# Low parts of weights made by an accumulating transfer in the mLSTM branch's projection

## The chip, the cores and the metric

The kernel runs on one core of one Trainium2 chip. The metric is device time in microseconds. The engines are TensorE (PE, with its weight loads as PEld), VectorE (DVE), ScalarE (ACT), GpSimd (POOL) and SyncE (SP), which here only issues transfers.

## What is computed

One layer of a streaming encoder on 256 tokens of width 2048. The input is normalised and goes through one wide projection. One branch is an mLSTM with 8 heads, the other a pooling mixer; each is multiplied by its own gate, projected back to 2048, and the two are merged by sigmoid gates. An output projection, a norm and the residual end the layer. The part that matters here is the first line below: `y_a` (256 x 2048) times `w_proj_mlstm` (2048 x 2048).

```
br_a = jnp.einsum('bsc,cd->bsd', y_a, w_proj_mlstm[l])
br_b = jnp.einsum('bsc,cd->bsd', y_b, w_proj_pool[l])
merged = jax.nn.sigmoid(g_a) * br_a + jax.nn.sigmoid(g_b) * br_b
out = jnp.einsum('bsd,de->bse', merged, w_out[l])
x = x + _rmsnorm(out, norm_post_w[l])
```

## The kernel before, in words

Every large product is made in three parts. Each factor is split into a high part (the value rounded to TensorE's float32r) and a low part (what is left), and high x high, low x high and high x low are summed in PSUM.

All weights stream from HBM. A raw tile of 128 x 2048 float32 (1 MB) is loaded by SP into one of three buffers (`rawp`, L49; the load is L102). It is cut into two halves of 1024 columns. For each half, `hi_lo` (L58) makes the high part `wh` by a copy on ACT (L61) and the low part `wl` by a subtraction on DVE, raw minus high (L62). `wh` and `wl` each have four buffers (`split`, L51), so ACT and DVE can be four halves ahead of PE, and a buffer comes free when PE has used it.

`tok_block` (L112) makes one 256 x 512 block of a product with tokens on the partitions: for each half first eight products with `wh` (L124 with the activations' high part, L125 with their low part), then four with `wl` (L127). The activations are the stationary operand. `chan_block` is its counterpart for products with channels on the partitions.

The order of the work is the order of the code: every engine runs its own queue in order and waits on semaphores for the others. Side jobs are generators that are advanced once per half (`step`, L78).

The last third of the kernel is a loop over four blocks of 512 output columns (j, L611). Each pass makes two gate blocks (L614, eight halves each), the pooling branch's projection (L625, four halves) and the mLSTM branch's projection (L630, four raw tiles, so eight halves), and then merges them on DVE (L635, L636). After the fourth pass comes the output projection (L684), whose weights have four further buffers for `wh` and `wl` in a pool of their own (`osplit`), so that ACT and DVE can start on them while PE is still in the fourth mLSTM projection.

GpSimd does little: constants at the start, the power -1/2 of the norms (L194, L666), and one addition for each token tile at the end (L672). Before the change no transfer is issued from it.

Of the kernel before, what the change touches and what calls it, by code (L numbers as in the profile page):

```python
# [10 lines left out]
F32 = mybir.dt.float32  # L11
F32R = mybir.dt.float32r
BF16 = mybir.dt.bfloat16
AF = mybir.ActivationFunctionType
ALU = mybir.AluOpType
AX = mybir.AxisListType

P = 128
# [20 lines left out]
def block_kernel(ctx: ExitStack, tc: tile.TileContext, a: dict, out: bass.AP):  # L39
# [3 lines left out]
    nc = tc.nc  # L43
# [5 lines left out]
    rawp = ctx.enter_context(tc.tile_pool(name="rawp", bufs=3, side="right"))  # L49
    gate = ctx.enter_context(tc.tile_pool(name="gate", bufs=2))  # L50
    split = ctx.enter_context(tc.tile_pool(name="split", bufs=4))  # L51
# [6 lines left out]
    def hi_lo(hi, lo, src, scale=None):  # L58

        if scale is None:  # L60
            nc.scalar.copy(hi, src)  # L61
            nc.vector.tensor_tensor(lo, src, hi.bitcast(F32), op=ALU.subtract)  # L62
        else:
            nc.scalar.activation(hi, src, AF.Copy, scale=scale)
            nc.vector.scalar_tensor_tensor(
                lo, src, scale, hi.bitcast(F32), op0=ALU.mult, op1=ALU.subtract
            )
# [10 lines left out]
    def step():  # L78
        side[:] = [g for g in side if next(g, None) is not None]

    def drain():
        while side:
            step()
# [14 lines left out]
    def w_tile(src, cuts=(0, 1024, 2048), pre=None, pool=split):  # L98

        raw = rawp.tile([P, 2048], F32, name="raw")  # L100
        if pre is None:
            nc.sync.dma_start(raw, src)  # L102
        for c0, c1 in zip(cuts, cuts[1:]):
            if pre is not None:
                pre(c0)
                nc.sync.dma_start(raw[:, c0:c1], src[:, c0:c1])
            wh = pool.tile([P, 1024], F32R, name="wh")
            wl = pool.tile([P, 1024], F32R, name="wl")
            hi_lo(wh[:, : c1 - c0], wl[:, : c1 - c0], raw[:, c0:c1])
            yield c0, c1, wh, wl  # L110

    def tok_block(tiles, st_h, st_l, opts=lambda kq: {}):  # L112

        ps = [acc.tile([P, 512], F32, name="acc") for _ in range(2)]
        n = 4 * len(tiles)
        for kq, src in enumerate(tiles):
            for c0, c1, wh, wl in w_tile(src, **opts(kq)):
                for part in range(2):
                    for c in range(c0, c1, 512):
                        k = kq * 4 + c // 512  # L120
                        cols = slice(c - c0, c - c0 + 512)
                        for t in range(2):
                            if part == 0:
                                nc.tensor.matmul(ps[t], st_h(k, t), wh[:, cols], start=k == 0, stop=False)  # L124
                                nc.tensor.matmul(ps[t], st_l(k, t), wh[:, cols], start=False, stop=False)  # L125
                            else:
                                nc.tensor.matmul(  # L127
                                    ps[t], st_h(k, t), wl[:, cols], start=False, stop=k == n - 1
                                )
                step()  # L130
        return ps
# [20 lines left out]
    def xtiles(b):  # L152
        return [a["wx"][b, i].rearrange("p k c -> p (k c)") for i in range(4)]
# [273 lines left out]

    side.append(stats())
    po = tok_block(xtiles(4), xh, xl, first)
    so0 = []  # L430
    for t in range(2):
# [12 lines left out]
    y_h = yp.tile([P, KT, T], F32R, name="y_h")  # L444
    y_l = yp.tile([P, KT, T], F32R, name="y_l")
# [119 lines left out]
    for j in range(4):  # L565
        po = tok_block(xtiles(4 + j), xh, xl) if j else so0
        so = []
        for t in range(2):
            s = gate.tile([P, 512], F32, name="g", tag=f"g{t}") if j else so0[t]
            nc.scalar.activation(s, po[t], AF.Sigmoid, scale=rstd[:, t : t + 1])  # L570
            so.append(s)
        pq = chan_block(qtiles(2 * j))
        drain()
        qh, ql, kh, kl = (
            ph1.tile([P, 4, T], F32R, name=n) for n in ("qh", "ql", "kh", "kl")
        )
        conv_block(pq, 4 * j, qh, ql, 0)
        pz = tok_block(xtiles(8 + j), xh, xl)
        for t in range(2):
            s = ph1.tile([P, 512], F32, name="sz", tag="sz", bufs=2)  # L580
            nc.scalar.activation(s, pz[t], AF.Sigmoid, scale=rstd[:, t : t + 1])
            nc.vector.scalar_tensor_tensor(s, pz[t], rstd[:, t : t + 1], s, op0=ALU.mult, op1=ALU.mult)
            nc.vector.tensor_tensor(so[t], so[t], s, op=ALU.mult)
        conv_block(chan_block(qtiles(2 * j + 1)), 4 * j + 2, qh, ql, 2)
        pv = tok_block(xtiles(j), xh, xl)
        for t in range(2):
            hi_lo(
                v_h[:, t, :, 0:HD], v_l[:, t, :, 0:HD], pv[t].rearrange("p (h d) -> p h d", h=2),
                rstd[:, t : t + 1],
            )  # L590
        conv_block(chan_block(qtiles(8 + 2 * j)), 16 + 4 * j, kh, kl, 0)
        conv_block(chan_block(qtiles(8 + 2 * j + 1)), 16 + 4 * j + 2, kh, kl, 2)
        side.append(mlstm_pair(j, so, (qh, ql, kh, kl)))


    def st(tile_):
        return lambda k, t: tile_[:, k, t * P : (t + 1) * P]
# [8 lines left out]
    def merges(j, ms):  # L606
        for t in range(2):
            yield 1
            merge(j, t, ms[t])

    for j in range(4):  # L611
        gs = []
        for n in range(2):
            pg = tok_block(xtiles(12 + 4 * n + j), xh, xl)  # L614
            for t in range(2):
                s = gate.tile([P, 512], F32, name="g", tag=f"g{t}")
                nc.scalar.activation(s, pg[t], AF.Sigmoid, scale=rstd[:, t : t + 1])
                gs.append(s)
        drain()
        if j == 0:  # L620
            ph1_ctx.close()
            late = ctx.enter_context(tc.tile_pool(name="late", bufs=1, side="right"))
            m_h = late.tile([P, KT, T], F32R, name="m_h")
            m_l = late.tile([P, KT, T], F32R, name="m_l")
        pb = tok_block(  # L625
            [a["wpp"][j, i].rearrange("p k c -> p (k c)") for i in range(2)], st(yb_h), st(yb_l)
        )
        for t in range(2):
            nc.vector.tensor_tensor(gs[2 + t], pb[t], gs[2 + t], op=ALU.mult)
        pa = tok_block(  # L630
            [a["wpm"][j, i].rearrange("p k c -> p (k c)") for i in range(4)], st(y_h), st(y_l)
        )
        for t in range(2):
            m = gs[t]
            nc.vector.tensor_tensor(m, pa[t], m, op=ALU.mult)  # L635
            nc.vector.tensor_tensor(m, m, gs[2 + t], op=ALU.add)  # L636
        side.append(merges(j, gs[:2]))
# [54 lines left out]
    for half in range(8):  # L692
        if half % 2 == 0:
            raw = rawp.tile([P, 2048], F32, name="raw")
            nc.sync.dma_start(raw, otiles(3)[half // 2])
        pool, bufs = (fin, 4) if half < 4 else (osplit, None)
        wh = pool.tile([P, 1024], F32R, name="wh", bufs=bufs)
        wl = pool.tile([P, 1024], F32R, name="wl", bufs=bufs)
        hi_lo(wh, wl, raw[:, half % 2 * 1024 : (half % 2 + 1) * 1024])
        ws.append((wh, wl))  # L700
    for t, parts in ((0, 1), (1, 2)):
        for part in range(parts):
            n = 512 // parts
            po = acc.tile([P, 512], F32, name="acc")[:, :n]
            for k in range(KT):
                wh, wl = ws[k // 2]
                cols = slice(k % 2 * 512 + part * n, k % 2 * 512 + (part + 1) * n)
                mm3(po, m_hi(k, t), m_lo(k, t), wh[:, cols], wl[:, cols], k == 0, k == KT - 1)
            c0 = 1536 + part * n
# [76 lines left out]
```

## Time and profile before

| | |
|---|---|
| median of 3 runs | 982.07 us (981.65 to 983.28) |
| profiled execution, its own time | 981.34 us |
| span of its instructions | 979.5 us |
| granted TensorE clock, mean | 0.997 |
| HBM read | 184.85 MB |

How to read the profile: "busy" is the time in which an engine executes, with its share of the span and the number of instructions. The chain is the work that ended last, followed back from the end. A row of instructions has the line of the kernel, the engine, the operation, output<-input by the program's names and the shape; in square brackets stands how long the engine was idle before it, and what ended that. A row of transfers has KB and the median time from issue to landing.

### The profile page before, as it was taken

Reading aid. Unit: us, or ns where it says so; the run is one execution under the profiler, and the core shown is the slowest. Engines: PE = TensorE matmul, PEld = TensorE weight load, DVE = VectorE, ACT = ScalarE, POOL = GpSimd, SP = SyncE. Lnnn points to the kernel's source line nnn. Section 1 sums busy time; section 2 is a strip of 40 time slices with the busy share of each in tenths; the row PEclk is TensorE's granted clock in tenths of the full one; section 3 lists DMA queues with packets and bytes.
Section 4 is the critical chain, followed back from the end, with each engine's and each line's share of the span. In section 5 each row is a group of like instructions: output and inputs, shape, how many; then the busy total and the mean of one; then the engine's idle time right before and its main releaser. Section 6 shows DMA issues by size and latency. Waiting matters only on the chain.

```text
span 979.5 us, 12387 instructions
## 1 busy us (share of the span) xinstructions
PE 967.9 (99%) x4801; PEld 817.9 (83%) x4801; DVE 626.9 (64%) x916; ACT 492.3 (50%) x664; POOL 14.5 (1%) x35
## 2 busy tenths in 40 slices
PE   8999999999999999999999999999999999999996
PEld 6888888888888888888888888888888888888886
DVE  7599776677766867758667686554454455455563
ACT  6757444456644565447544465444434434443451
POOL 1000000000000000000000000000000000000001
PEclk9999999999999999999999999999999999999998
DMA  8855554554455436463555544555555555566542
GB/s 313 308 207 207 180 170 177 204 182 172 142 205 209 176 130 215 172 214 132 182 202 178 209 172 149 196 192 194 173 186 200 207 180 189 197 254 262 177 168 86
DMA packets 29162, 187.74 MB, mean 192 GB/s; under 512 B 3248, under 2 KB 4016, under 8 KB 7600
## 3 DMA queue, kind: packets, MB, share of 16 engines
q1 hardware_dynamic: 28672, 183.81, 52.7%
q10 hardware_dynamic: 432, 3.15, 0.8%
q8 instruction: 37, 0.61, 0.3%
q14 instruction: 21, 0.17, 0.1%
HBM read 184.85 MB, written 2.10 MB: 191 GB/s over the span
## 4 chain that ended last, share of the span: by engine, by line
PE 97%; issue 1%; DMA 1%; SPq 0%; ACT 0%; POOL 0%; DVE 0%; DVEq 0%; ACTq 0%; POOLq 0%
PE acc L124 21%; PE acc L125 21%; PE acc L127 21%; PE acc L144 18%; PE acc L146 9%; PE sm L71 1%; PE sm L72 1%; PE sm L70 1%; DMA raw<-in_wx 1%; PE sm L287 0%; PE acc L70 0%; PE acc L72 0%; PE acc L71 0%; PE sm L556 0%; PE sm L602 0%
## 5 line engine op out<-in xcount | busy, mean ns | idle before, releaser
L62 DVE TENSOR_TENSOR wl<-raw,wh 128x1024 fp32r<-128x1024 f32 (+1 forms) x338 | 409.0, 1217 | 276.3 <-ACT wh L61 274.3
L61 ACT CAST wh<-raw 128x1024 fp32r<-128x1024 f32 (+1 forms) x338 | 351.2, 1046 | 371.1 <-PE acc L125 248.2
L124 PE MATMUL acc<-wh,xc 128*128 128x512 f32 x640 | 251.5, 393 | 1.6 <-ACT wh L61 1.6
L125 PE MATMUL acc<-wh,xc 128*128 128x512 f32 x640 | 249.7, 390 | 0.0
L144 PE MATMUL acc<-xc,wh 128*128 128x512 f32 x768 | 193.0, 394 | 0.9 <-ACT wh L61 0.9
L127 PE MATMUL acc<-wl,xc 128*128 128x512 f32 x640 | 171.6, 390 | 0.0
L144 PEld LDWEIGHTS acc<-xc,wh 128*128 128x128 f32 x768 | 138.8, 189 | 26.8 <-ACT wh L61 1.3
L124 PEld LDWEIGHTS acc<-wh,xc 128*128 128x128 f32 x640 | 120.3, 188 | 26.6 <-ACT wh L61 3.1
L127 PEld LDWEIGHTS acc<-wl,xc 128*128 128x128 f32 x640 | 120.2, 188 | 25.2
L125 PEld LDWEIGHTS acc<-wh,xc 128*128 128x128 f32 x640 | 120.3, 188 | 23.9
L146 PEld LDWEIGHTS acc<-xc,wl 128*128 128x128 f32 x768 | 104.8, 190 | 7.5
L146 PE MATMUL acc<-xc,wl 128*128 128x256 f32 x768 | 107.1, 283 | 0.0
L124 PE MATMUL acc<-wh,y_h 128*128 128x512 f32 x128 | 49.9, 390 | 0.0
L125 PE MATMUL acc<-wh,y_l 128*128 128x512 f32 x128 | 49.8, 389 | 0.0
L474 DVE SCALAR_TENSOR_TENSOR cy<-pad,vec,cy 128x256 f32<-128x256 f32 x96 | 39.3, 479 | 0.0
L124 PE MATMUL acc<-wh,m_h 128*128 128x512 f32 x96 | 37.6, 392 | 0.0
L125 PE MATMUL acc<-wh,m_l 128*128 128x512 f32 x96 | 37.4, 390 | 0.0
L127 PE MATMUL acc<-wl,y_h 128*128 128x512 f32 x128 | 34.2, 390 | 0.0
L125 PEld LDWEIGHTS acc<-wh,y_l 128*128 128x128 f32 x128 | 24.0, 188 | 5.0
L127 PEld LDWEIGHTS acc<-wl,y_h 128*128 128x128 f32 x128 | 24.0, 188 | 5.0
L124 PEld LDWEIGHTS acc<-wh,y_h 128*128 128x128 f32 x128 | 24.0, 188 | 5.0
L127 PE MATMUL acc<-wl,m_h 128*128 128x512 f32 x96 | 25.7, 390 | 0.0
(188 smaller groups left out, 752.0 us busy)
## 6 DMA issues: line engine op xcount, KB each, us to landing
raw<-in_wx SPq DMA_DIRECT2D x76, 1024.0 KB, 4.8
raw<-in_wq SPq DMA_DIRECT2D x48, 1024.0 KB, 4.8
raw<-in_wpm SPq DMA_DIRECT2D x16, 1024.0 KB, 4.8
raw<-in_wo SPq DMA_DIRECT2D x16, 1024.0 KB, 4.8
raw<-in_wpp SPq DMA_DIRECT2D x8, 1024.0 KB, 4.7
raw<-in_wx SPq DMA_DIRECT2D x6, 512.0 KB, 6.9
xt<-in_x SPq DMA_DIRECT2D x4, 512.0 KB, 5.8
xr<-in_x ACTq DMA_DIRECT2D x2, 1024.0 KB, 7.9
```

What stands on the lines that cost most here:

```text
L61: nc.scalar.copy(hi, src)
L62: nc.vector.tensor_tensor(lo, src, hi.bitcast(F32), op=ALU.subtract)
L70: nc.tensor.matmul(ps, lh, rh, start=start, stop=False)
L71: nc.tensor.matmul(ps, ll, rh, start=False, stop=False)
L72: nc.tensor.matmul(ps, lh, rl, start=False, stop=stop)
L124: nc.tensor.matmul(ps[t], st_h(k, t), wh[:, cols], start=k == 0, stop=False)
L125: nc.tensor.matmul(ps[t], st_l(k, t), wh[:, cols], start=False, stop=False)
L127: nc.tensor.matmul(ps[t], st_h(k, t), wl[:, cols], start=False, stop=k == n - 1)
L144: nc.tensor.matmul(ps[c], wh[:, cols], xc[:, k], start=k == 0, stop=False)
L146: nc.tensor.matmul(ps[c][:, 1], wl[:, cols], xc[:, k, 0], start=False, stop=k == KT - 1)
L474: nc.vector.scalar_tensor_tensor(y, pad[:, 1 + j : 1 + j + T], cw[:, j : j + 1], y, op0=ALU.mult, op1=ALU.add)
```

## The change

In the mLSTM branch's projection alone, the second half of each raw tile is split in another way. ACT copies the high part as before. Then ACT writes the negated high part into `wl`, and GpSimd issues a transfer from the weights in HBM to `wl` that adds what it reads to what is there: the weights plus the negated high part. The first half of each tile is split as before. There are four tiles in each of four blocks, so this concerns 16 halves: h1, h3, h5 and h7 of each block, counting from h0. The lines behind L111 move down by 15.

```diff
+    def w_tile_acc(src, pool=split):
+
+        raw = rawp.tile([P, 2048], F32, name="raw")
+        nc.sync.dma_start(raw, src)
+        for c0, c1 in ((0, 1024), (1024, 2048)):
+            wh = pool.tile([P, 1024], F32R, name="wh")
+            wl = pool.tile([P, 1024], F32R, name="wl")
+            if c0 == 0:
+                hi_lo(wh, wl, raw[:, c0:c1])
+            else:
+                nc.scalar.copy(wh, raw[:, c0:c1])
+                nc.scalar.mul(wl, wh.bitcast(F32), -1.0)
+                nc.gpsimd.dma_start(wl, src[:, c0:c1], accum_op=ALU.add)
+            yield c0, c1, wh, wl
...
-    def tok_block(tiles, st_h, st_l, opts=lambda kq: {}):
+    def tok_block(tiles, st_h, st_l, opts=lambda kq: {}, tile_of=None):
...
-            for c0, c1, wh, wl in w_tile(src, **opts(kq)):
+            for c0, c1, wh, wl in (tile_of or w_tile)(src, **opts(kq)):
...
         pa = tok_block(
-            [a["wpm"][j, i].rearrange("p k c -> p (k c)") for i in range(4)], st(y_h), st(y_l)
+            [a["wpm"][j, i].rearrange("p k c -> p (k c)") for i in range(4)], st(y_h), st(y_l), tile_of=w_tile_acc
         )
```

The first place is ACT's queue at the start of the first block. In the rows, the numbers behind wh, wl and raw count tiles of the program; in brackets stand the queues that the instruction waits for (DMAHW a load, DMASW a transfer issued from GpSimd). Before:

```order
L61 CAST wh_5611<-raw_5609 128x1024 [waits DMAHW2_49,DVE_49,PE_49]
L61 CAST wh_5627<-raw_5609 128x1024 [waits DVE_49,PE_49]
L61 CAST wh_5645<-raw_5643 128x1024 [waits DMAHW3_49,DVE_49,PE_49]
L61 CAST wh_5661<-raw_5643 128x1024 [waits DVE_49,PE_49]
L61 CAST wh_5679<-raw_5677 128x1024 [waits DMAHW4_49,DVE_49,PE_49]
L61 CAST wh_5695<-raw_5677 128x1024 [waits DVE_49,PE_49]
```

The same place of the same queue in the changed program:

```order
L61 CAST wh_5611<-raw_5609 128x1024 [waits DMAHW2_49,DVE_49,PE_49]
L122 CAST wh_5627<-raw_5609 128x1024 [waits DVE_49,PE_49]
L123 ACTIVATE wl_5628<-wh_5627 128x1024 [waits PE_49,Activation_49]
L61 CAST wh_5646<-raw_5644 128x1024 [waits DMAHW3_49,DVE_49,PE_49]
L122 CAST wh_5662<-raw_5644 128x1024 [waits DVE_49,PE_49]
L123 ACTIVATE wl_5663<-wh_5662 128x1024 [waits PE_49,Activation_49]
L61 CAST wh_5681<-raw_5679 128x1024 [waits DMAHW4_49,DVE_49,PE_49]
L122 CAST wh_5697<-raw_5679 128x1024 [waits PE_49]
L123 ACTIVATE wl_5698<-wh_5697 128x1024 [waits DMASW0_49,PE_49,Activation_49]
```

Behind the second copy of each tile stands the negation (L123), which waits for PE to give back the buffer of wl and for ACT's own copy.

The second place is ACT's queue at the end of the fourth block, where the copies of the output projection's weights (raw_7305 and raw_7346 before, raw_7321 and raw_7362 after) stand between those of the mLSTM projection. Before:

```order
L61 CAST wh_7231<-raw_7213 128x1024 [waits DVE_49,PE_49]
L61 CAST wh_7307<-raw_7305 128x1024 [waits DMAHW0_49]
L61 CAST wh_7249<-raw_7247 128x1024 [waits DMAHW7_49,DVE_49,PE_49]
L61 CAST wh_7323<-raw_7305 128x1024
L61 CAST wh_7265<-raw_7247 128x1024 [waits DVE_49,PE_49]
L61 CAST wh_7348<-raw_7346 128x1024 [waits DMAHW1_49]
L61 CAST wh_7371<-raw_7346 128x1024
```

The same place in the changed program:

```order
L122 CAST wh_7245<-raw_7227 128x1024 [waits PE_49]
L61 CAST wh_7323<-raw_7321 128x1024 [waits DMAHW0_49]
L123 ACTIVATE wl_7246<-wh_7245 128x1024 [waits DMASW4_49,PE_49,Activation_49]
L61 CAST wh_7264<-raw_7262 128x1024 [waits DMAHW7_49,DVE_49,PE_49]
L61 CAST wh_7339<-raw_7321 128x1024
L122 CAST wh_7280<-raw_7262 128x1024 [waits PE_49]
L61 CAST wh_7364<-raw_7362 128x1024 [waits DMAHW1_49]
L123 ACTIVATE wl_7281<-wh_7280 128x1024 [waits DMASW5_49,PE_49,Activation_49]
L61 CAST wh_7387<-raw_7362 128x1024
```

Here the negations of h5 (wl_7246) and h7 (wl_7281) stand one copy behind their high parts, after a copy that waits for a load of the output projection's weights.

The third place is GpSimd's queue from the last norm of the mLSTM on, in the changed program. Before, L666 (now L681) followed directly on that norm.

```order
L209 TENSOR_TENSOR rs_5342<-rs_tmp_5343,mhalf_111 128x2 [waits DVE_49]
L124 DMA wl_5628<-in_wpm 128x1024 [waits DVE_49,Activation_49]
L124 DMA wl_5663<-in_wpm 128x1024 [waits DVE_49,Activation_49]
L124 DMA wl_5698<-in_wpm 128x1024 [waits DMASW0_49,Activation_49]
L124 DMA wl_5733<-in_wpm 128x1024 [waits DMASW1_49,Activation_49]
L124 DMA wl_6144<-in_wpm 128x1024 [waits DMASW2_49,DVE_49,Activation_49]
```

These are the first five of the sixteen transfers; each waits for ACT's negation, and no other work of GpSimd stands between the first and the last.

## The prediction

> **What bounds the kernel now.** I read the page's busy times and chain first, then the table of windows over the four stages that the change edits, then the timelines of PE, ACT and DVE inside one of them.
>
> ```profile
> span 979.5 us, 12387 instructions
> PE 967.9 (99%) x4801; PEld 817.9 (83%) x4801; DVE 626.9 (64%) x916; ACT 492.3 (50%) x664; POOL 14.5 (1%) x35
> PE 97%; issue 1%; DMA 1%; SPq 0%; ACT 0%; POOL 0%; DVE 0%; DVEq 0%; ACTq 0%; POOLq 0%
> ```
>
> PE is busy for 967.9 of 979.5 us and makes 97% of the chain. The four runs of the mLSTM projection (one for each j) lie in these stretches; after the times come busy us of PE, PEld, DVE, ACT and POOL, the clock, the DMA share and GB/s:
>
> ```profile
> 629.60:651.40 21.80, 21.80 (x98) 18.02 (x97) 11.03 (x11) 8.44 (x9) 0.00 (x0) 1.00 0.53 193
> 706.60:728.30 21.70, 21.70 (x98) 17.96 (x97) 11.00 (x10) 8.35 (x9) 0.00 (x0) 1.00 0.54 192
> 783.50:805.30 21.80, 21.80 (x98) 18.07 (x97) 11.00 (x10) 8.45 (x9) 0.00 (x0) 1.00 0.54 192
> 860.70:882.50 21.80, 21.80 (x98) 18.05 (x97) 11.87 (x11) 8.75 (x9) 0.00 (x0) 1.00 0.66 252
> ```
>
> PE is busy in every microsecond of all four, at full clock, with DVE about half busy and ACT less. So nothing taken from DVE can shorten these stages; the change can only leave them as they are or open a wait on PE. The whole question is whether the new low parts arrive in time.
>
> A half tile (1024 columns, eight products with wh, then four with wl) takes PE 21.75 / 8 = 2.72 us. I number the halves of a block h0 to h7; the change edits h1, h3, h5 and h7. Two of PE's groups with wl, those of h1 and h5 in the second block:
>
> ```profile
> 711.28 1.07 PE L127 MATMUL acc<-wl,y_h 128*128 128x512 f32 x4
> ...
> 722.17 1.07 PE L127 MATMUL acc<-wl,y_h 128*128 128x512 f32 x4
> ```
>
> Of wl there are four buffers, so h5 writes the buffer that h1's group gives back at 711.28 + 1.07 = 712.35, and PE asks for it at 722.17. ACT's and DVE's share of it now:
>
> ```profile
> 711.48 1.05 ACT L61 CAST wh<-raw 128x1024 fp32r<-128x1024 f32 x1 [1.67 <-PE acc L125]
> 714.21 1.05 ACT L61 CAST wh<-raw 128x1024 fp32r<-128x1024 f32 x1 [1.67 <-PE acc L125]
> 712.57 1.23 DVE L62 TENSOR_TENSOR wl<-raw,wh 128x1024 fp32r<-128x1024 f32 x1 [1.49 <-ACT wh L61]
> ```
>
> ACT copies h5's high part at 711.48, DVE has the low part ready at 712.57 + 1.23 = 713.80: 8.37 us before it is used. That lead is what the change spends.
>
> **What goes.** Sixteen subtractions on DVE (four in each block) of 1.23 us, 19.7 us of DVE. DVE is not on the chain in these stages, so this is worth 0. With them goes DVE as the last reader of the raw tile: SP's next load waits for ACT's copy of h5 (done at 712.53) instead of DVE (713.80), about 1.3 us sooner. No PE wait is due to a load here, so that is 0 too.
>
> **What comes on ACT.** Sixteen negations of 128x1024. No such row exists; the nearest is the CAST of the same shape, 1.05 us, and a longer or shorter one moves the sum by the same amount. It must wait for wl's buffer (712.35) and for the copy before it (712.53), so it runs from 712.53 to about 713.58. Queued behind it on ACT is h6's copy, which cannot start before 714.21: the negation fits into the 1.67 us that ACT idles between copies, with 0.6 us to spare. Price 0; if it were 0.6 us longer, the next copy would slip, and that copy has DVE's 8 us lead before PE sees it.
>
> **What comes on GpSimd and the DMA engines.** Sixteen accumulating transfers of 512 KB, each waiting for ACT's negation. GpSimd's own work around them:
>
> ```profile
> 597.14 0.69 POOL L194 TENSOR_TENSOR rs<-rs_tmp,mhalf 128x2 f32<-128x2 f32 x1 [4.37 <-DVE rs_tmp L193]
> 961.43 0.55 POOL L666 TENSOR_TENSOR rs<-rs,mhalf 128x1 f32<-128x1 f32 x1 [363.60 <-DVE rs L665]
> 962.81 1.76 POOL L672 TENSOR_TENSOR xr<-ob,xr 128x512 f32<-128x512 f32 x1 [0.83 <-ACT ob L671]
> ```
>
> From 597.83 to 961.43 it does nothing, so no transfer stands behind other work, and behind the waiting transfers stand only each other and L666, 79 us after the last block. Then PE's first product with that wl waits for the transfer, and behind this wait stands all of PE's queue.
>
> The budget D, from the end of the negation until the data has landed: 722.17 - 713.58 = **8.6 us**. In the last block it is less, because there ACT also copies the output projection's weights between h5's copy and h5's negation (the second piece of the order), and these copies wait for loads:
>
> ```profile
> 865.72 1.05 ACT L61 CAST wh<-raw 128x1024 fp32r<-128x1024 f32 x1 [1.67 <-PE acc L125]
> 868.12 4.09 ACT L61 CAST wh<-raw 128x1024 fp32r<-128x1024 f32 x4 [1.35 <-DMA raw<-in_wo]
> 876.40 1.07 PE L127 MATMUL acc<-wl,y_h 128*128 128x512 f32 x4
> ```
>
> With its load freed earlier I put that copy right behind h5's at 866.77, so h5's negation ends at 866.77 + 2 x 1.05 = 868.87, and 876.40 - 868.87 = **7.5 us** are left; the same shift holds for h7.
>
> D has no row: no accumulating transfer and none from GpSimd is in the trace. The nearest rows (share of 16 engines; issues with KB and median us to landing):
>
> ```profile
> q1 hardware_dynamic: 28672, 183.81, 52.7%
> raw<-in_wpm SPq DMA_DIRECT2D x16, 1024.0 KB, 4.8
> xr<-in_x ACTq DMA_DIRECT2D x2, 1024.0 KB, 7.9
> ```
>
> A load of 1.049 MB occupies all 16 engines for 0.527 x 979.5 x 1.049 / 183.81 = 2.94 us; it lands after 4.8, so 1.86 us are fixed. An accumulating transfer of half the size reads the weights and the old contents of wl, so it moves between 1.47 us' worth (the second read free) and 2.94 (both reads in turn); I take 2.94, since the engine must have both before it can write. GpSimd's share before the data starts: between 0 and the longest GpSimd row, 1.76; I take 1.0, the middle. Company: SP's raw load of the same pair is issued about 1 us before the transfer; the two xr loads, issued together, took 7.9 - 4.8 = 3.1 us longer than a lone load; I take 1.0, the part of a 2.94 us load that is still running when the transfer starts some 2 us later. D = 1.0 + 1.86 + 2.94 + 1.0 = **6.8 us**. By the low ends it is 1.86 + 1.47 = 3.3, by the high ends 1.76 + 1.86 + 2.94 + 3.1 = 9.7. Nothing in the trace shows the pace of the addition; were it to double the moving part again, the high end is 12.6.
>
> The Trainium skill, "Collectives: The Full Stack", section "The bandwidth ceiling: the fold count and why AG ≠ RS ≠ AR", says that a transfer that adds is half as fast as a copy because it needs two source reads, and not because the addition costs cycles. By that rule D is the 6.8 above; with the second read free it would be 5.3. No run here shows either yet.
>
> 6.8 lies inside 8.6 and inside 7.5, so PE waits for nothing. If D is larger: PE stalls at h1 by D - 8.6; h3's buffer was free before that stall, so h3 arrives in time; h5 waits again, h7 not. Two stalls a block, so the time lost is 6 x (D - 8.6) + 2 x (D - 7.5), each term counted from zero.
>
> **The sum.** Profiled execution 981.34 us (span 979.5, 1.84 around it), change 0. The median of the three runs, 982.07, is 0.73 above the profiled one. My forecast is 982.1. 0.2% of it, 2 us, is about what a measurement of this kernel can tell from no change; by the formula D = 8.5 is where it is passed.
>
> **Rivals.**
> *A, the transfer comes late (slower).* A single mechanism: the low part of h1 and h5 lands after PE asks for it, in all four blocks. It decides from D = 8.5 up. At D = 9.7 it costs 6.6 + 4.4 = 11 us (993), at 11.5 it costs 17.4 + 8 = 25 (1007.5), at 12.6 24 + 10.2 = 34 (1016). For it: only 1.7 us lie between my D and the budget, less than the 3.1 us by which company lengthened the xr loads, and GpSimd's share is a guess. Against it: every high end must come together for 9.7.
> *B, the DMA engines are full (slower by more).* The addition doubles the moving part to 5.88 us. Together with the raw load that is 8.82 us of engine time per pair of halves, in which PE needs 5.44: 3.4 us short each pair, 13.5 a block. The 1.8 us between 6.8 and 8.6, about 2, absorb some in each block: 4 x 11.5 = 46 us, some 1028. For it: the windows show 0.53 in use already, and 0.53 + 5.88/5.44 is 1.6. Against it: with one count per read, 0.53 + 0.54 = 1.07 only just fills the engines, and over a block of 22 us the 1.5 us short are covered by the budget. By the Trainium skill's rule above B would not occur.
> *C, a gain.* It would need PE time in these blocks to give back, and there is none; PE's 11.6 idle us lie elsewhere. Only the spread of the runs (981.65 to 983.28) could look like one.
>
> **How the numbers follow.** No change 0.56: the central D and its low end lie inside, the high end of the rows does not. A 0.28, B 0.12, C 0.04. Slower by over 0.2% is A and B, 0.40; faster 0.04. The range: from 980.5, the median less most of 0.2%, up to D = 11.5 in A, 1007.5; that leaves out B (0.12), the upper end of A (0.06) and half of C (0.02). The likeliest case alone spans 980.5 to 984.
>
> **What would show it.** Right: the four windows again show PE at 21.7 to 21.8 us without a wait, the transfers land within 8.6 us of the negation's end (7.5 in the last block), DVE has 16 subtractions fewer and ACT 16 instructions of about 1.05 us more. A: PE waits on the transfer at h1 and h5, eight times, each by the same length. B: a DMA share near 1.0 in the windows, every accumulating transfer later than the one before. Wrong altogether: any change of time with PE's windows unchanged.

## The result, and the profile after

The changed kernel takes 991.84 us (median of 4 runs, 989.75 to 995.48) against 981.9 us before: 1.0106 times as long, 95% interval 1.0091 to 1.012. The time lies in the range, but the likeliest case, no change, was wrong. Rival A came true in kind: PE waits for the transfers, though mostly at other halves, and not for equal lengths. (Ratios here and below are those of the timed comparison; they can differ a little from the ratio of the medians.)

The page of the changed kernel, in its profiled execution of 990.87 us: span, busy times, the queue of the transfers issued from GpSimd, the chain, and these transfers' path from issue to landing (median, us).

```profile
span 988.0 us, 12422 instructions
PE 970.8 (98%) x4801; PEld 818.6 (83%) x4801; DVE 607.7 (62%) x900; ACT 509.3 (52%) x680; POOL 28.6 (3%) x51
q0 software_dynamic: 2304, 8.39, 4.7%
PE 91%; DMA 5%; issue 1%; ACT 1%; SPq 1%; DVE 0%; POOL 0%; DVEq 0%; ACTq 0%; POOLq 0%
wl<-in_wpm POOLq DMA_DIRECT2D x16, 512.0 KB, 7.2
```

DVE has sixteen instructions and 19 us fewer, ACT sixteen and 17 us more, as costed. New is DMA in the chain, 5%. The four stretches of the mLSTM projection, by windows (times, length, busy us of PE, PEld, DVE, ACT and POOL, clock, DMA share, GB/s):

```profile
629.80:652.00 22.20, 22.20 (x98) 18.03 (x97) 7.58 (x8) 11.73 (x12) 2.60 (x3) 1.00 1.00 266
707.20:731.10 23.90, 22.42 (x98) 18.02 (x97) 7.59 (x8) 11.69 (x12) 2.60 (x3) 1.00 0.97 260
786.30:808.20 21.90, 21.90 (x98) 18.15 (x97) 7.56 (x8) 11.66 (x12) 2.60 (x3) 1.00 0.98 276
863.40:889.60 26.20, 22.20 (x98) 17.99 (x97) 8.69 (x9) 11.32 (x12) 2.61 (x3) 1.00 0.94 277
```

The DMA share has gone from 0.53 to nearly 1. The blocks are not hit alike: the third is as long as before, the second 2 us and the fourth 4.3 us longer (from the first product's start to the last one's; the windows are rounded outwards to 0.1 us). Where, the timeline of PE says, with the groups of wl at h5 of the second block and at h7 of the fourth, each with its idle time:

```profile
724.46 1.20 PE L142 MATMUL acc<-wl,y_h 128*128 128x512 f32 x4 [1.48 <-DMA wl<-in_wpm]
...
888.46 1.20 PE L142 MATMUL acc<-wl,y_h 128*128 128x512 f32 x4 [4.00 <-DMA wl<-in_wpm]
```

The halves are placed by ACT's timeline, whose negations (L123) are h1, h3, h5 and h7 of a block in turn; of the fourth block also the copies (L61) of the output projection's weights, with what they waited for:

```profile
713.03 1.06 ACT L123 ACTIVATE wl<-wh 128x1024 fp32r<-128x1024 f32 x1
...
870.25 1.05 ACT L61 CAST wh<-raw 128x1024 fp32r<-128x1024 f32 x1 [1.05 <-DMA raw<-in_wo]
871.20 1.06 ACT L123 ACTIVATE wl<-wh 128x1024 fp32r<-128x1024 f32 x1
...
876.21 1.05 ACT L61 CAST wh<-raw 128x1024 fp32r<-128x1024 f32 x1 [1.11 <-DMA raw<-in_wo]
877.16 1.05 ACT L123 ACTIVATE wl<-wh 128x1024 fp32r<-128x1024 f32 x1
```

D, from the end of the negation until PE goes on, was 724.46 - 714.09 = 10.4 us at h5 of the second block and 888.46 - 878.21 = 10.3 at h7 of the fourth. The path from issue to landing varies between the sixteen transfers (the view by tile; us):

```profile
DMA to landing us min/median/max: 6.1/7.2/10.0
```

GpSimd issues 0.3 us after the negation ends (0.45 in the row below), so D is 7.5 in the median and about 10.4 at worst. GpSimd's timeline for the last transfer:

```profile
878.66 0.88 POOL L124 DMA_DIRECT2D wl<-in_wpm  x1 [5.25 <-ACT wl L123]
```

While this transfer waited, the DMA engines carried loads alone. The queues from 879.6 to 882.8, packets, MB and share of the 16 engines:

```profile
q1 hardware_dynamic: 161, 1.17, 102.3%
raw<-in_wo SPq DMA_DIRECT2D x1, 1024.0 KB, 8.6
```

q1 is SP's queue; q0 has no packet there. For 3.2 us after it was issued the transfer moved nothing, while the loads for the output projection filled the engines. Then both queues moved, from 882.85 to 887.75:

```profile
q0 software_dynamic: 142, 0.52, 53.7%
q1 hardware_dynamic: 138, 1.02, 50.4%
```

So this path of 9.75 us is made of GpSimd's instruction (0.88), 3.3 us without a packet, 4.9 us of moving at half the engines, and 0.66 until it has landed. The packets of all sixteen show the same parts: from GpSimd's instruction to the first packet 2.0 us in the median, from first to last packet 4.2, though the packets of one by themselves hold the engines for 2.85. One transfer, the third of the fourth block, found the engines mostly free, and its first packet came after 0.72 us. By this reading the difference is what the loads add.

The stall has an echo. The window behind it, where PE is never idle:

```profile
889.70:893.10 3.40, 3.40 (x9) 2.63 (x8) 2.25 (x4) 0.00 (x0) 0.00 (x0) 0.50 0.72 226
```

The granted clock is 0.50 for 3.4 us, which costs half of that, 1.7 us. The balance of this execution, by the same measure as above: the blocks are 0.3 + 2.0 + 0 + 4.3 = 6.6 us longer, the clock adds 1.7, together 8.3 of the span's 8.5 us.

### The profile page after: what moved, and what is told of

The parts are those of the page before. It is cut to its first block, busy times and chain, and to the rows that moved or that the text cites. A ratio compares the mean times of both kernels' runs of the same rounds, so it can differ in the third digit from the quotient of the medians.

```text
span 988.0 us, 12422 instructions
## 1 busy us (share of the span) xinstructions
PE 970.8 (98%) x4801; PEld 818.6 (83%) x4801; DVE 607.7 (62%) x900; ACT 509.3 (52%) x680; POOL 28.6 (3%) x51
## 4 chain that ended last, share of the span: by engine, by line
PE 91%; DMA 5%; issue 1%; ACT 1%; SPq 1%; DVE 0%; POOL 0%; DVEq 0%; ACTq 0%; POOLq 0%
PE acc L139 20%; PE acc L140 20%; PE acc L142 20%; PE acc L159 18%; PE acc L161 9%; DMA wl<-in_wpm 2%; PE sm L71 1%; PE sm L72 1%; PE sm L70 1%; DMA raw<-in_wq 1%; DMA raw<-in_wo 1%; DMA xt<-in_x 1%; DMA raw<-in_wx 1%; PE sm L302 0%; PE acc L70 0%
## 5 line engine op out<-in xcount | busy, mean ns | idle before, releaser
L62 DVE TENSOR_TENSOR wl<-raw,wh 128x1024 fp32r<-128x1024 f32 (+1 forms) x322 | 389.7, 1216 | 299.0 <-ACT wh L61 294.0
L61 ACT CAST wh<-raw 128x1024 fp32r<-128x1024 f32 (+1 forms) x322 | 334.4, 1045 | 330.5 <-PE acc L140 211.8
L122 ACT CAST wh<-raw 128x1024 fp32r<-128x1024 f32 x16 | 16.8, 1049 | 25.1 <-PE acc L140 25.1
```

Source lines behind the costliest of these rows:

```text
L122: nc.scalar.copy(wh, raw[:, c0:c1])
```

## The experiments

Theory P: most of the loss arises in the fourth block, where the negations of h5 and h7 stand behind copies that wait for the output projection's loads, and where these loads stand ahead of the transfers. Rival Q: the DMA engines are full, and every block loses alike.

**One block or three.** Two kernels with the change in a part of the blocks.

```diff
-            [... "wpm" ...], st(y_h), st(y_l), tile_of=w_tile_acc
+            [... "wpm" ...], st(y_h), st(y_l), tile_of=w_tile_acc if j < 3 else None
```

> The change in the first three blocks only; the fourth splits its weights as before. Theory P (the place: most of the loss arises in the fourth block, where the negations of h5 and h7 stand behind copies that wait for the output projection's loads): PE's windows of the changed kernel lost 0.28, 1.96 and 0 us in these blocks, so about 984 us (982 to 986). Rival Q (the transfer engines are full, every block loses alike): three quarters of 9.9 us, about 989.4 us.

Measured: 984.3 us against 981.92, ratio 1.0033 (1.0019 to 1.0047).

```diff
+            [... "wpm" ...], st(y_h), st(y_l), tile_of=w_tile_acc if j == 3 else None
```

> The change in the fourth block only. Theory P: the 4.3 us of PE's stall in that block and the 1.7 us of the halved clock behind it, about 988 us (986 to 990). Rival Q: a quarter of 9.9 us, about 984.5 us.

Measured: 988.11 us, ratio 1.0066 (1.0052 to 1.0081). So some 2.4 us belong to the first three blocks and 6.2 to the fourth; together 8.6 of the 9.9. P holds, and Q's equal shares fall. The parts agree less well than the sums. In the profiled execution of the first kernel the three blocks are only 1.1 us longer, nearly all in the third; the rest of its loss lies at the kernel's start (see the end of the next section). In the profiled execution of the second kernel PE waited at h5 and h7 of the fourth block, 4.5 us in all, and the clock was not halved, so that there the loss is not made of the 4.3 and 1.7 us that were expected:

```profile
878.55 1.19 PE L142 MATMUL acc<-wl,y_h 128*128 128x512 f32 x4 [1.66 <-DMA wl<-in_wpm]
...
887.09 1.19 PE L142 MATMUL acc<-wl,y_h 128*128 128x512 f32 x4 [2.80 <-DMA wl<-in_wpm]
```

**The changed kernel once more**, to see what a second execution does.

> The changed kernel once more. Theory P: 989 to 993 us; PE loses most in the fourth block (4 to 5 us, at h5 and h7) and 0 to 2 us in the first three together, at other halves than in the first profile. Rival Q: the same loss in every block.

Measured: 992.65 us, ratio 1.0107 (1.0089 to 1.0125). PE waits at the same two halves, h5 of the second block and h7 of the fourth, and for shorter times at h5 of the first and h3 of the fourth:

```profile
646.37 1.21 PE L142 MATMUL acc<-wl,y_h 128*128 128x512 f32 x4 [0.64 <-DMA wl<-in_wpm]
...
725.63 1.39 PE L142 MATMUL acc<-wl,y_h 128*128 128x512 f32 x4 [1.81 <-DMA wl<-in_wpm]
...
877.00 1.21 PE L142 MATMUL acc<-wl,y_h 128*128 128x512 f32 x4 [0.67 <-DMA wl<-in_wpm]
...
892.22 2.07 PE L142 MATMUL acc<-wl,y_h 128*128 128x512 f32 x4 [4.00 <-DMA wl<-in_wpm]
```

The third block is again free, and h7 of the fourth again the worst. The first three blocks lost more than expected here, 4.7 us, of which 1.7 come from a halved clock behind the wait of 1.81 us.

**The order at the fourth block.** The output projection's first block takes its buffers from the mLSTM projection's pool, so that its copies follow the last negation on ACT, and its loads come later.

```diff
-        po = tok_block(otiles(j), st(m_h), st(m_l), lambda kq: {"pool": osplit})
+        po = tok_block(otiles(j), st(m_h), st(m_l), lambda kq: {"pool": split if j == 0 else osplit})
```

> The change in all four blocks, but the first block of the output projection takes its wh and wl from the same four buffers as the mLSTM projection. Its copies then stand behind the last negation on ACT, and its loads come later. Theory P: the fourth block loses no more than the others, up to 2 us, and the clock is not halved: 984 to 986 us. Rival Q: nothing changes in the engines' load, 990 us or more.

Measured: 986.0 us, ratio 1.0044 (1.0029 to 1.0058). Six of the ten us are gone, and the halved clock with them. The edit moves the copies and the loads together, so it does not tell which of the two counts. In the fourth block one wait is left:

```profile
879.84 1.20 PE L142 MATMUL acc<-wl,y_h 128*128 128x512 f32 x4 [1.15 <-DMA wl<-in_wpm]
```

**Late negation or loads ahead?** In the fourth block alone the negation moves from ACT to DVE, where h5's need not wait for the output projection's first load; the loads stay.

```diff
-                nc.scalar.mul(wl, wh.bitcast(F32), -1.0)
+                nc.vector.tensor_scalar(wl, wh.bitcast(F32), -1.0, None, op0=ALU.mult)
```

> The change in the fourth block only, with the negation on DVE instead of ACT. On DVE the negation of h5 stands ahead of the output projection's first subtractions, so it need not wait for that load; it ends about 2 us sooner, that of h7 about 1.5 us sooner. If the late negation is what costs the fourth block its 6 us: 983 to 985 us, no stall at h5 and 1 to 2 us at h7. If it is the loads ahead of the transfers: 986 to 988 us, as with the negation on ACT.

Measured: 984.44 us against 981.68, ratio 1.0025 (1.0014 to 1.0035), so 2.8 us instead of 6.2. The place was not as expected: h7 is in time, and h5 is the one that waits. Its negation by ACT (fourth block alone), by DVE, and PE's wait behind the latter:

```profile
869.00 1.06 ACT L123 ACTIVATE wl<-wh 128x1024 fp32r<-128x1024 f32 x1
```

```profile
866.71 0.69 DVE L123 TENSOR_SCALAR wl<-wh 128x1024 fp32r<-128x1024 f32 x1 [1.50 <-ACT wh L122]
```

```profile
878.03 1.19 PE L142 MATMUL acc<-wl,y_h 128*128 128x512 f32 x4 [1.57 <-DMA wl<-in_wpm]
```

The negation ends at 867.40 instead of 870.06, but D is 878.03 - 867.40 = 10.6 us. So both are at work: with the earlier negation a little more than half of the fourth block's loss is gone, and a transfer that takes 10.6 us makes the rest. That the loads are what lengthens it is read from the packets and not shown by a kernel without them: this transfer had its first packet 2.4 us after GpSimd's instruction and then moved for 6.45 us, of which loads took half the engines' time and its own packets 3.2 us.

**A plain copy.** The transfer does not add.

```diff
-                nc.gpsimd.dma_start(wl, src[:, c0:c1], accum_op=ALU.add)
+                nc.gpsimd.dma_start(wl, src[:, c0:c1])
```

> As the change, but GpSimd's transfers copy the weights into wl without adding (the low parts are then the weights themselves; the negation stays, so the timing of issue is the same). If the second read is what makes the transfer late (a 4 KB packet took 0.33 us, as long as an 8 KB packet of a load): the transfer moves in about 1.5 us instead of 2.9, the DMA share in the windows falls from 0.97 to about 0.8, blocks one to three lose nothing and the fourth 0 to 3 us: 982 to 985 us. If it is only that GpSimd issues it and that loads stand ahead of it: as the change, 989 to 993 us.

Measured: 983.72 us, ratio 1.0019 (1.0008 to 1.0029). Its transfers: the queue, the path, and the DMA share in the first block.

```profile
q0 software_dynamic: 2304, 8.39, 2.6%
wl<-in_wpm POOLq DMA_DIRECT2D x16, 512.0 KB, 5.6
```

```profile
630.80:652.70 21.90, 21.90 (x98) 18.16 (x97) 7.55 (x8) 11.66 (x12) 1.62 (x3) 1.00 0.79 269
```

A copy holds all engines for 0.026 x 982.2 us, divided by 16 transfers, = 1.60 us; the adding transfer for 0.047 x 988.0 / 16 = 2.90, 1.8 times as long. The Trainium skill ("Collectives: The Full Stack", "The bandwidth ceiling: the fold count and why AG ≠ RS ≠ AR") lays a halved rate to the second source read; this factor agrees. The first three blocks lose nothing, the fourth 1.3 us. Of the change's 9.9 us the copy keeps 1.8, so most of the loss comes with the adding and not with the issue through GpSimd as such. The path is 1.6 us shorter: 0.33 in GpSimd's instruction (0.54 instead of 0.87) and 1.3 in the engines' time.

**Half the size.** The transfer makes 512 of the 1024 columns, DVE the others.

```diff
+                nc.vector.tensor_tensor(
+                    wl[:, :512], raw[:, c0 : c0 + 512], wh[:, :512].bitcast(F32), op=ALU.subtract
+                )
-                nc.scalar.mul(wl, wh.bitcast(F32), -1.0)
-                nc.gpsimd.dma_start(wl, src[:, c0:c1], accum_op=ALU.add)
+                nc.scalar.mul(wl[:, 512:], wh[:, 512:].bitcast(F32), -1.0)
+                nc.gpsimd.dma_start(wl[:, 512:], src[:, c0 + 512 : c1], accum_op=ALU.add)
```

> Of each second half only 512 columns are made by the transfer (256 KB); DVE subtracts the other 512. If the size of the transfer makes it late: it moves in about 1.5 us instead of 2.9, the first three blocks lose nothing and the fourth 0 to 2 us: 982 to 985 us, like the plain transfer. If the fixed path through GpSimd and the loads ahead make it late: 987 us or more.

Measured: 986.56 us, ratio 1.0043 (1.0029 to 1.0058), a miss: between the two expectations. Its path:

```profile
q0 software_dynamic: 2304, 4.20, 2.5%
wl<-in_wpm POOLq DMA_DIRECT2D x16, 256.0 KB, 6.9
```

The engines are held for half as long (0.025 x 982.5 / 16 = 1.53 us), yet the path is 6.9 instead of 7.2. An adding transfer of 256 KB, which holds the engines as long as the plain one of 512 KB, lands 1.3 us later than that (6.9 against 5.6). A longer fixed part is not the reason. Where no load is ahead, the first packet comes 0.7 to 0.9 us after GpSimd's instruction (h3 of each block), as with the one full transfer above; in the other halves it comes after 3.0 to 3.9 us, behind loads. Nor is an early start a gain, as the transfer of h3 in the second block shows. These are the queues from its first packet to its last, 710.14 to 714.79:

```profile
q1 hardware_dynamic: 132, 1.05, 59.0%
q0 software_dynamic: 131, 0.26, 33.1%
```

It needs 4.65 us for work of 1.56, because a whole load passes beside it. The negation is shorter here (0.63 us), so the transfers are issued sooner and meet the loads at another point; that this is why the gain is so small is argued, not shown. Its profiled execution lost 2.3 us, all in the fourth block; the other runs, up to 988.12, have no profile, so what they lost is open.

**Five buffers.** The pool of wh and wl gets one more buffer, 2.72 us more time for each transfer.

```diff
-    split = ctx.enter_context(tc.tile_pool(name="split", bufs=4))
+    split = ctx.enter_context(tc.tile_pool(name="split", bufs=5))
```

> The change with five buffers for wh and wl instead of four: 2.72 us more between the negation and PE's use. The program's order also differs at the end of the fourth block: both negations stand ahead of the output projection's copies, and these stand behind the loads of post and xr. If the transfer is only too late by its time of 7 to 10 us against 8.6: no stall in any of the four blocks; 982 to 983 us, or about 984 if PE then waits for the output projection's first copy. If the DMA engines are too slow for the sum of the bytes: the stalls stay, 988 us or more.

Measured: 984.41 us, ratio 1.0025 (1.0017 to 1.0034). No wait on a transfer is left, though the path is no shorter (median 7.8, at most 10.3). PE's new wait, right behind the fourth block:

```profile
887.42 1.23 PE L617 MATMUL sm<-ident,g 128*128 128x128 f32 x8 [1.84 <-DVE g L651]
```

The program's order now has the merge's transposes ahead of the output projection's first products. The next kernel joins this with the edit of the order above.

> Five buffers for wh and wl, and the first block of the output projection takes its buffers from the same pool, so that PE's queue has the merge's transposes behind the output projection's first halves again, as before the change. If the 2.5 us that five buffers alone still lost are PE's wait for the merge (1.8 us) and the transfer itself is fully covered: 982 to 983 us, no wait on a transfer. If something else of the transfer costs them: 984 us or more.

Measured: 982.61 us against 981.68, ratio 1.0012 (1.0003 to 1.0021). Its waits of PE are those of the kernel's start, none on a transfer, with landings as late as before (view by tile):

```profile
DMA to landing us min/median/max: 6.5/8.2/10.6
```

So nearly all that the change costs is that the transfer comes too late, not that it happens: 0.9 us are left of 9.9. The old kernel with five buffers was not run, so what these buffers do by themselves is not known.

**Twice the transfers.** Both halves are made by the negation and the transfer.

```diff
-            if c0 == 0:
-                hi_lo(wh, wl, raw[:, c0:c1])
-            else:
-                nc.scalar.copy(wh, raw[:, c0:c1])
-                nc.scalar.mul(wl, wh.bitcast(F32), -1.0)
-                nc.gpsimd.dma_start(wl, src[:, c0:c1], accum_op=ALU.add)
+            nc.scalar.copy(wh, raw[:, c0:c1])
+            nc.scalar.mul(wl, wh.bitcast(F32), -1.0)
+            nc.gpsimd.dma_start(wl, src[:, c0:c1], accum_op=ALU.add)
```

> Both halves of each tile of the mLSTM projection are made by the negation and the transfer: twice the transfers. If a transfer takes 2.9 us of all 16 engines: a block needs 8 x 2.9 + 4 x 2.9 = 35 us of them against PE's 21.8, so each block is some 11 to 13 us longer, 1028 to 1036 us, and DMA share in the blocks is 1.0. If the engines are no limit and only the path of about 7.5 us counts: under 1000 us.

Measured: 1016.83 us, ratio 1.0353 (1.0339 to 1.0366), between the two. The first two blocks by windows:

```profile
629.60:660.20 30.60, 24.86 (x98) 18.86 (x97) 5.21 (x6) 14.00 (x14) 4.32 (x5) 0.94 0.99 270
715.40:744.80 29.40, 23.74 (x98) 17.73 (x97) 5.19 (x6) 14.02 (x14) 4.33 (x5) 1.00 1.03 282
```

Here the engines are the limit (share 0.99 to 1.03, these two blocks 8.8 and 7.7 us longer). My number was too high. The queue's share in this kernel was 8.5% of the engines' span for 32 transfers, 0.085 x 1015.4 / 32 = 2.70 us each, and of the eight transfers of a block the first runs ahead of it: 7 x 2.70 + 4 x 2.94 = 30.7, which meets the first block's 30.6. This sum was made after the result, and the second block is already shorter. That is how rival B looks. With half the transfers, 4 x 2.90 + 4 x 2.94 = 23.4 us of work stand against a block of 21.8: the engines are just over full, and the lead covers most of it.

## Why the prediction was right or wrong

*The range and the likeliest case:* the measured time lies in the range, but the central case, no wait at all, was wrong. Rival A's price for D = 9.7, 993 us, is close by luck: it adds eight equal waits. What came were two waits of 1.5 and 4.0 us (four in the second profile) and a halved clock, of which no term of the sum or of A spoke.

*What bounds the kernel, and what goes and comes on DVE and ACT:* right. Taking 19 us from DVE gave nothing; a negation takes 1.06 us (forecast 1.05).

*The transfer's parts:* the engines are held for 2.90 us (forecast 2.94). GpSimd's share and the fixed part were forecast at 1.0 + 1.86 = 2.86 and are about 1.9 where no load is in the way: 0.87 for the instruction, 0.72 to the first packet, 0.3 from the last packet to the landing. So they were too large by about 1 us.

*Company, "I take 1.0":* this step failed. A path of 7.2 in the median gives D 7.5 against 6.8, near the forecast and inside 8.6, but by luck: with the measured parts a transfer without loads beside it takes 0.3 + 0.87 + 0.72 + 2.9 + 0.3 = 5.1 us, so the loads add 2.4 in the median and not 1.0, and the excess in the fixed part hides most of that. And I set one value for sixteen transfers where the range decides. D reached 10.4, so that the loads added 5.3 us, beyond the 3.1 us of the xr row, which I had put at the far end. I had let the transfer wait for the rest of one load; the packets show that it also shares the engines with the next one while it moves. Each wait of PE comes from such a transfer, not from a typical one. My formula of two equal stalls in each block was wrong for the same reason: in the two executions of the changed kernel h1 never made PE wait, h5 did so in the second block both times and in the first block once, and the third block never stalled.

*The last block, "7.5 us are left":* too long. I had the load of the output projection land as early as an undisturbed one; the transfer of h3 runs beside it, and it took 6.4 us instead of 4.7. ACT's copies waited 1.05 us for it and 1.11 us for a later load, and the negation of h7 ended at 878.21. PE would have asked for it at 884.30 (the last product with wh starts at 884.07, 0.23 us before), which leaves 6.1 us. The change delays its own start there. Moving the copies behind the negation, and with them the loads, brought the kernel from 991.84 to 986.0.

*The order of the work:* it was described above as that of the code. The copies of the output projection stand among those of the fourth block because the program's scheduler draws them forward into free buffers, not because the code is written so; with buffers from the shared pool they stood behind the last negation.

*Rival B:* the share is near 1 as its line said, and in two blocks a backlog does grow: the paths of h1, h3, h5 and h7 are 6.6, 8.3, 8.0, 8.3 us in the first block and 6.9, 8.2, 10.0, 8.6 in the second. In the third they stay at 6.1 to 6.5; why, nothing here shows. The doubling of the moving part that B needs did not come (2.90 us). Only with twice the transfers did the engines set the length of a block.

*The chances:* 0.56 on no change rested on a margin of 1.7 us, against landings that range over 3.9 (6.1 to 10.0). The xr row's 3.1 us, taken as a scatter instead of as a bound, would have made A the likeliest.

One thing stays open. The first block of the mLSTM projection began between 629.5 and 631.3 us in the profiled executions of kernels with four buffers, which are alike up to there; this scatter of 1.8 us lies in all differences of 1 to 2 us. It arises in the first 45 us: PE waits there for ACT's copies for 1.8 us in the shortest case (twice the transfers) and 4.4 in the longest (first three blocks), and the full clock begins between 4.3 and 6.4 us. By my estimate from these two, with half of the clock's delay counted, the starts agree to within some 0.3 us; why they vary is not shown.

## What to carry to other kernels

A transfer that must arrive before a busy engine asks for it is judged by the latest of its kind, not by the median: compare the lead with the longest landing under the loads of that very stage, and look for stages in which later loads are drawn forward. Where work from an engine that is half idle goes to a path that is seven times as long (1.23 us on DVE, 1.06 + 0.3 + 7.2 on the new path), there is nothing to win if that engine was not on the chain; here it took one more buffer, and an edit of the order behind the fourth block, to lose next to nothing. A late operand costs more than its own wait when the wait also lets TensorE's clock fall.

## What the runs showed of the hardware that I had not expected

A transfer issued from GpSimd did not share the engines evenly with queued loads: for 3.2 us it moved nothing while SP's queue held 102% of them. An adding transfer and a copy of the same 512 KB differ in two parts: GpSimd's instruction is 0.87 us against 0.54, and the engines are held for 2.90 us against 1.60. The rest is alike: from the instruction's end to the first packet 0.72 us at the shortest in both, and 2.0 to 2.2 in the median, behind loads.

The clock fell to 0.50 for 3.4 us behind a wait of 4.00 us, but also once behind one of 1.81 us (the changed kernel's second profile), while waits of 1.66 and 2.80 us (fourth block alone) and of 2.06 us (half the size) left it at 1.00. The Trainium skill ("TensorE: Matmul & The Clock Gate", "Part 1: The HAM clock gate (the "warmup" mystery)") gives half clock after at least one idle window of about 3.4 us, and says that the window runs freely. The length of the halved stretch agrees with it, and so does a wait of 4.00 us taken by its length; the wait of 1.81 us does not. The window behind that wait:

```profile
726.50:729.80 3.30, 3.30 (x9) 2.54 (x8) 1.23 (x1) 0.00 (x0) 0.00 (x0) 0.50 0.34 60
```

Where a wait lies counts more than its length. The clock's changes in these traces fall on steps of 3.413 us: in the changed kernel at 889.68, 893.10 and 981.84 us, one step and 26 steps apart. Seven times in all the profiled executions the clock fell between the start and the end of the kernel, and each time PE had waited at least 1.81 us within the step that then ended. The wait of 2.80 us was cut by a step's end into 1.32 and 1.48, and even that of 4.00 us did not fill a whole step (1.82 and 2.19). Waits of 1.81 to 1.95 us within one step went either way, and 2.09 or more always let it fall. This is read from the traces; no kernel was made to test it.
